# A small product moved from VectorE to GpSimd, transposes placed later among gate products, and a shorter conv norm sequence in a hybrid attention and convolution layer

## The chip, the cores and the metric

The kernel runs on one core of one Trainium2 chip. The metric is the device time of one execution in microseconds (us); lower is better. Engines are TensorE (matmuls and transposes, PE in the profile), VectorE (DVE), ScalarE (ACT), GpSimd (POOL) and SyncE (SP, which starts the DMAs).

## The reference

One pre-norm layer on x of 512 rows by 1024 columns, all float32. What the change touches lies in the token mixing:

```python
h = rms_norm(x, norm1_g)
proj = h @ w_in            # q, three K/V pairs, branch gates, conv input, merge gates
# compressed branch: softmax over 31 compressed keys, weighted by its branch gate
p_c = softmax(q . kc * scale - slope * dist) * valid ;  o_c = p_c @ vc
# selected and window branch (here all blocks are chosen: both are causal attention over 512 keys)
o = g0 * o_c + g1 * o_s + g2 * o_w ;   y_attn = o @ w_attn_br
# convolution branch
z = a * sigmoid(gate) ;  z = causal_dwconv(z, width 31) + b
z = silu(layer_norm(z)) ;  y_conv = z @ w_conv_br
x = x + (sigmoid(g_a) * y_attn + sigmoid(g_b) * y_conv) @ w_out
```

A gated convolution FFN and a final RMSNorm follow.

## The kernel before

Activations are held transposed, in 128 by 512 tiles. Every float32 operand is split into a rounded high part and a low part; a product is three matmuls, high by high (line 285), high weight by low activation (288) and low weight by high activation (291), each of 128x512. The weights' high parts are made by ScalarE (line 91) and the low parts by GpSimd or VectorE (line 93, tiles `wl`), from `raw` tiles that SyncE loads.

The attention runs in **16 steps** (lines 832 to 865): 8 heads by two branches, b = 0 for selected and b = 1 for window. Step s holds, on TensorE: `qk(s, 3)`, `qk(s, 2)` and `qk(s, 1)`, the scores of four row blocks (lines 739 and 744); `pv(s - 2)`, the value products (781, 786); and `ptr(s - 1, ...)`, the transposes of the probabilities of the step before, in three batches (768). Between them `fill(n)` puts n matmuls of the 480 of the merge gates' projection and of the convolution's output projection (`filler`, lines 605 to 615). TensorE's order is the order of the code (`manual_schedule`); the other engines' orders are set by a scheduler.

Behind each score tile VectorE finds the row maximum and subtracts (line 725, tile `p`), ScalarE takes the exponential and its sum (727), VectorE inverts the sum (754), and GpSimd scales the probabilities by it and by the branch gate (758, `soft`). Transposed probabilities leave their bank by ScalarE (771, `pt..h`) and VectorE (772, `pt..l`). Banks are few: two for scores (`s`), two for transposes (`t`), two for gate products (`mm`), one each for `o` and `y`. So the third batch of a step's transposes waits until both engines have emptied the bank of the first.

The compressed branch has its softmax in `cmp_scores` (lines 449 to 472), called for two halves before the steps: VectorE adds the distances, takes maxima and sums, inverts the sum (467) and multiplies it by the branch gate (470, `cst<-cst,gate`, 128x16); GpSimd applies the slope (464) and that product (471); ScalarE takes the exponential (465). `cmp_T` (474 to 484) transposes the result for four heads at a time, through the `t` banks (lines 479, 482, 483, tiles `pct`); both calls stand in step 2.

The convolution's 31 taps are VectorE work (508), fed out by `side(s)`, which is called six times a step. From step 6 on `side` advances `conv_norm` (645 to 691) by one `yield` per call: sums over channels (634 to 638), a mean by matmul (651), centring and squares (655, 656), sums of squares, a variance by matmul (663), a power on GpSimd (667), a scale spread by matmul (674), scaling (678 to 684) and the tiles `cB` (688, 689) that the convolution's output projection (`cb`) reads. Loops of empty `yield`s between them put calls between a VectorE result and the matmul that reads it.

Of the kernel before, what the change touches and what calls it, by code (L numbers as in the profile page):

```python
# [11 lines left out]
ALU = mybir.AluOpType  # L12
# [103 lines left out]
def hybrid_block_kernel(ctx: ExitStack, tc: tile.TileContext, x, norm1_g, w_in, cmp_pe_k, cmp_pe_v,  # L116
# [8 lines left out]
    act, vec, pool = nc.scalar, nc.vector, nc.gpsimd  # L125
# [6 lines left out]
    def big(name, shape=(P, 2, S), dt=F32):  # L132
        return sp.tile(list(shape), dt, tag="s", name=name)
# [140 lines left out]
    def psum(tag, name, pl=None):  # L274
        return psB.tile([P, S], F32, tag=tag, name=name, bufs=NB[tag])
# [173 lines left out]
    def cmp_scores(ib):  # L449
        pc = big(f"pc{ib}", (P, 2, 8, 32))  # L450
        st = bp.tile([P, 3, 16], F32, tag="cst", name=f"cst{ib}", bufs=2)
        pcf = pc.rearrange("p i h n -> p (i h) n")
        for ii in range(2):
            i = 2 * ib + ii
            ps = psum("st"[ib], f"sc{i}")
            pv = ps.rearrange("p (h a n) -> p h a n", h=8, a=2)
            for h in range(NH):
                mm(pv[:, h].rearrange("p a n -> p (a n)"), lhsT=QS[h // 2][:, h % 2, i * P : (i + 1) * P],
                   rhs=kc[:, h // 4].rearrange("p a n -> p (a n)"), start=True, stop=True)
            vec.tensor_tensor(pc[:, ii], pv[:, :, 1], ndc[:, i].unsqueeze(1).broadcast_to([P, 8, 32]), op=ALU.add)  # L460
            vec.tensor_tensor(pc[:, ii], pv[:, :, 0], pc[:, ii], op=ALU.add)
        vec.tensor_reduce(st[:, 0], pcf, axis=AX.X, op=ALU.max)
        vec.tensor_tensor(pcf, pcf, st[:, 0].unsqueeze(2).broadcast_to([P, 16, 32]), op=ALU.subtract)
        pool.tensor_tensor(pc, pc, sl.unsqueeze(1).unsqueeze(3).broadcast_to([P, 2, 8, 32]), op=ALU.mult)
        act.activation(pc, pc, AF.Exp)
        vec.tensor_reduce(st[:, 1], pcf, axis=AX.X, op=ALU.add)
        vec.reciprocal(st[:, 2], st[:, 1])
        gv = gate[:, 2 * ib : 2 * ib + 2].rearrange("p i (h b) -> p i h b", b=3)[:, :, :, 0]
        s2 = st[:, 2].rearrange("p (i h) -> p i h", i=2)
        vec.tensor_tensor(s2, s2, gv, op=ALU.mult)  # L470
        pool.tensor_tensor(pcf, pcf, st[:, 2].unsqueeze(2).broadcast_to([P, 16, 32]), op=ALU.mult)
        PC.append(pc)

# [2 lines left out]
    def cmp_T(hg):  # L476
        ps = psum("t", f"pct{hg}")
        for i in range(4):
            tr(ps[:, i * P : (i + 1) * P],
               PC[i // 2][:, i % 2, 4 * hg : 4 * hg + 4].rearrange("p h n -> p (h n)"), ident)  # L480
        pt_ = big(f"pct{hg}", dt=F32R)
        act.copy(pt_[:, 0], ps)
        vec.tensor_tensor(pt_[:, 1], ps, pt_[:, 0].bitcast(F32), op=ALU.subtract)
        PCT.append(pt_)
# [56 lines left out]
    for u in range(2):  # L541
        for i in range(2):
# [4 lines left out]
            for e in range(2):  # L547
                a, b = slice(64 * e, 64 * e + 64), slice(64 - 64 * e, 128 - 64 * e)
# [9 lines left out]
    for b in range(2):  # L558
# [4 lines left out]
        for g in range(2):  # L563
            kk = big(f"kk{b}{g}", dt=F32R)
            a, o_ = slice(64 * g, 64 * g + 64), slice(64 - 64 * g, 128 - 64 * g)
# [52 lines left out]
    left = [480]  # L618

    def fill(n):  # L620
        for _ in range(min(n, left[0])):
            next(fg)
            left[0] -= 1
# [21 lines left out]
    def conv_norm():  # L645

        yield from csum("sum")
        for _ in range(5):
            yield
        ps = psum("y", "cmean")  # L650
        mm(ps, lhsT=ones, rhs=cv["sum"], start=True, stop=True)
        yield
        for c in range(4):
            with pin():
                vec.tensor_tensor(zy[c][:, 0], zy[c][:, 1], ps, op=ALU.subtract)
                act.activation(zy[c][:, 1], zy[c][:, 0], AF.Square)
            yield
        yield from csum("sq")
        for _ in range(5):
            yield  # L660
        ps = psum("y", "cvar")
        for t in range(4):
            mm(ps[:, 2 * t : 2 * t + 2], lhsT=cv["sq"][:, t * P : (t + 1) * P], rhs=ones[:, 0:2], start=True, stop=True)
        rt = bp.tile([P, 8], F32, tag="crt", name="crt")
        dg = big("cdg", (P, 4, P))
        act.activation(rt, ps[:, :8], AF.Identity, bias=cst[:, 0:1])
        pool.tensor_tensor(rt, rt, cst[:, 1:2].broadcast_to([P, 8]), op=ALU.pow)
        for t in range(4):
            vec.tensor_scalar(dg[:, t], ident, rt[:, 2 * t : 2 * t + 1], 512.0, op0=ALU.mult, op1=ALU.mult)
        for _ in range(4):  # L670
            yield
        rs = psum("y", "crs")
        for t in range(4):
            mm(rs[:, t * P : (t + 1) * P], lhsT=ones, rhs=dg[:, t], start=True, stop=True)
        yield
        for c in range(4):
            with pin():
                vec.tensor_tensor(zy[c][:, 0], rs, zy[c][:, 0], op=ALU.mult)
                act.activation(zy[c][:, 0], zy[c][:, 0], AF.Identity, scale=lnh[:, c : c + 1],
                               bias=lnh[:, 4 + c : 5 + c])  # L680
            yield
            with pin():
                act.activation(zy[c][:, 1], zy[c][:, 0], AF.Tanh)
                vec.scalar_tensor_tensor(zy[c][:, 1], zy[c][:, 1], 1.0, zy[c][:, 0], op0=ALU.add, op1=ALU.mult)
            yield
            cb = big(f"cB{c}", dt=F32R)
            with pin():
                act.copy(cb[:, 0], zy[c][:, 1])
                pool.tensor_tensor(cb[:, 1], zy[c][:, 1], cb[:, 0].bitcast(F32), op=ALU.subtract)
            cB.append(cb)  # L690
            yield
# [138 lines left out]
    cmp_scores(1)  # L830
    fill(16)
    for s in range(16):
        n = left[0] - left[0] * (15 - s) // (16 - s) - (6 if s == 2 else 0)
        a = n // 4
        if s >= 1:
            soft(s - 1)
        qk(s, 3)
        side(s)
        fill(a - 1 if s else a + 2)
        qk(s, 2)  # L840
        side(s)
        fill(a if s else a + 6)
        qk(s, 1)
        side(s)
        if s >= 2:
            pv(s - 2)
        if s in (1, 9):
            padded(s // 9)
        if s == 2:
            cmp_T(0)  # L850
            fill(3)
            cmp_T(1)
            fill(3)
        if s >= 1:
            ptr(s - 1, [0])
        side(s)
        fill(a if s else 0)
        if s >= 1:
            ptr(s - 1, [1])
        side(s)  # L860
        fill(a if s else 0)
        if s >= 1:
            ptr(s - 1, [2, 3])
        side(s)
        fill(n - 4 * a + 1 if s else n - 2 * a - 8)
    assert left[0] == 0 and next(fg, None) is None and len(sig) == 16 and next(cn, None) is None


# [141 lines left out]
    for p in range(11):  # L1010
        tmp = {}
        for br, nm in enumerate("av"):
            tl = fp.tile([P, 2, S], F32, tag="ft", name=f"f{nm}{p}", bufs=3)
            tmp[nm] = tl
            for i in range(2):
# [9 lines left out]
                else:  # L1025
                    a = tmp["a"][:, i]
# [56 lines left out]
```

## Time and profile before

| | us |
|---|---|
| median of 3 runs (lowest to highest) | 748.64 (746.31 to 748.89) |
| the profiled execution's own time | 746.94 |
| its span in the trace | 745.2 |
| TensorE busy in the span | 727.0 |
| VectorE, ScalarE, GpSimd busy | 440.5, 335.8, 216.8 |

In the views below, a time is us from the span's start; a timeline row gives start and length of a run of equal instructions, how many there are, and in brackets how long the engine had been idle and on whom it waited. Matmuls are pipelined and their ends are modelled, so a run of equal matmuls is given with the modelled length of its last one; a single gate product of 128x512 is given as 0.39. PEclk is the clock granted to TensorE as a share of its full 2.4 GHz.

### The profile page before, as it was taken

How to read it: one execution, taken by the hardware profiler on the slowest of the kernel's cores; microseconds unless marked ns; L12 is line 12 of the kernel's file. 1: busy time of each engine (PE TensorE's matmuls, PEld its weight loads, DVE VectorE, ACT ScalarE, POOL GpSimd, SP SyncE). 2: the span in 40 equal slices, each digit the busy share in tenths (PEclk: the TensorE clock that was granted, in tenths of full speed). 3: DMA queues.
4: the chain of work that ended last, by engine and by line, in shares of the span. 5: the costliest groups of instructions: out<-in, count | busy, mean ns of one | idle time of the engine just before them, and what ended most of it. 6: DMA issues, size and time to landing. Idle time of an engine off the chain costs nothing.

```text
span 745.2 us, 9261 instructions
## 1 busy us (share of the span) xinstructions
PE 727.0 (98%) x3583; PEld 612.7 (82%) x3583; DVE 440.5 (59%) x755; ACT 335.8 (45%) x592; POOL 216.8 (29%) x168
## 2 busy tenths in 40 slices
PE   7999999889999999999999999999999999999995
PEld 7988889778878878788898888888888888888884
DVE  5479899989965656450358565656656564212225
ACT  6522576456567865342156434444443443112113
POOL 6544666565356664177330000000000000000001
PEclk9999999999999999999999999999999999999998
DMA  7442434211111111243433313322361332233102
GB/s 237 137 135 76 139 98 147 72 58 58 57 56 58 57 58 57 85 168 115 151 133 113 113 59 111 113 96 76 113 226 60 110 113 90 79 113 113 57 2 113
DMA packets 58613, 74.90 MB, mean 101 GB/s; under 512 B 2017, under 2 KB 48457, under 8 KB 58569
## 3 DMA queue, kind: packets, MB, share of 16 engines
q1 hardware_dynamic: 58569, 74.31, 29.9%
q8 instruction: 28, 0.46, 0.2%
q14 instruction: 16, 0.13, 0.1%
HBM read 70.11 MB, written 4.19 MB: 100 GB/s over the span
## 4 chain that ended last, share of the span: by engine, by line
PE 62%; issue 1%; DVE 0%; ACT 0%; POOLq 0%; POOL 0%
PE d0acc L936 16%; PE o0acc L936 6%; PE uv L285 5%; PE uv L291 5%; PE uv L288 5%; PE ua L291 5%; PE ua L285 5%; PE ua L288 5%; PE cb L291 1%; PE ab L885 1%; PE ab L889 1%; PE ab L887 1%; PE cb L288 1%; PE cb L285 1%; PE o L781 1%; PE t L768 1%
## 5 line engine op out<-in xcount | busy, mean ns | idle before, releaser
L91 ACT CAST wh<-raw 128x1024 fp32r<-128x1024 f32 (+1 forms) x114 | 117.5, 1036 | 195.9 <-PE d0acc L936 69.5
L93 DVE TENSOR_TENSOR wl<-raw,wh 128x1024 fp32r<-128x1024 f32 x62 | 75.7, 1223 | 129.3 <-PE d0acc L936 68.3
L93 POOL TENSOR_TENSOR wl<-raw,wh 128x1024 fp32r<-128x1024 f32 (+1 forms) x52 | 121.3, 2343 | 105.5 <-ACT wh L91 39.4
L1049 POOL TENSOR_TENSOR mf<-mf,cst 128x1 f32<-128x1 f32 x4 | 3.7, 931 | 356.1 <-DVE mf L1047 356.1
L936 PE MATMUL d0acc<-wh,act 128*128 128x512 f32 x352 | 86.9, 389 | 0.0
L508 DVE SCALAR_TENSOR_TENSOR cy<-zy,colB,cy 128x482 f32<-128x482 f32 (+28 forms) x116 | 85.0, 733 | 3.0 <-ACT cy L502 1.1
L936 PEld LDWEIGHTS d0acc<-wh,act 128*128 128x128 f32 x352 | 66.1, 188 | 13.7
L727 ACT ACTIVATE p<-p,st 128x512 f32<-128x512 f32 (+3 forms) x64 | 35.6, 558 | 28.9 <-DVE st L725 28.9
L936 PE MATMUL d0acc<-wl,act 128*128 128x512 f32 x176 | 47.0, 389 | 0.0
L285 PE MATMUL uv<-h,wh 128*128 128x512 f32 x176 | 44.4, 389 | 0.0
L758 POOL TENSOR_SCALAR p<-p,st,gate 128x512 f32<-128x512 f32 (+3 forms) x60 | 36.7, 630 | 25.4 <-DVE st L754 23.8
L288 PE MATMUL uv<-h,wh 128*128 128x512 f32 x176 | 43.5, 389 | 0.0
L291 PE MATMUL uv<-h,wl 128*128 128x512 f32 x176 | 43.5, 389 | 0.0
L285 PE MATMUL ua<-h,wh 128*128 128x512 f32 x160 | 39.5, 389 | 0.0
L291 PE MATMUL ua<-h,wl 128*128 128x512 f32 x160 | 39.5, 389 | 0.0
L288 PE MATMUL ua<-h,wh 128*128 128x512 f32 x160 | 39.5, 389 | 0.0
L288 PEld LDWEIGHTS uv<-h,wh 128*128 128x128 f32 x176 | 33.0, 188 | 6.9
L936 PEld LDWEIGHTS d0acc<-wl,act 128*128 128x128 f32 x176 | 33.0, 188 | 6.9
L291 PEld LDWEIGHTS uv<-h,wl 128*128 128x128 f32 x176 | 33.0, 188 | 6.9
L285 PEld LDWEIGHTS uv<-h,wh 128*128 128x128 f32 x176 | 32.6, 188 | 6.4
L285 PE MATMUL g<-h,wh 128*128 128x512 f32 x128 | 37.7, 417 | 0.0
L725 DVE CUSTOM_DVE_ANT_0 p<-s,nd 128x512 f32<-128x512 f32 (+3 forms) x64 | 29.8, 486 | 12.9 <-PE s L739 10.0
(386 smaller groups left out, 1438.7 us busy)
## 6 DMA issues: line engine op xcount, KB each, us to landing
raw<-in_ffn_w_up_dram SPq DMA_DIRECT2D x22, 1024.0 KB, 4.9
raw<-in_w_in_dram SPq DMA_DIRECT2D x11, 1024.0 KB, 4.9
raw<-in_ffn_w_down_dram SPq DMA_DIRECT2D x11, 1024.0 KB, 4.7
raw<-in_w_in_dram SPq DMA_DIRECT2D x10, 512.0 KB, 3.7
raw<-in_w_out_dram SPq DMA_DIRECT2D x4, 1024.0 KB
x<-in_x_dram SPq DMA_DIRECT2D x4, 512.0 KB, 7.2
raw<-in_w_conv_br_dram SPq DMA_DIRECT2D x2, 1024.0 KB, 4.8
raw<-in_w_attn_br_dram SPq DMA_DIRECT2D x2, 1024.0 KB
```

The source lines that it names most:

```text
L91: nc.scalar.copy(wh, src)
L93: eng.tensor_tensor(wl, src, wh.bitcast(F32), op=ALU.subtract)
L285: mm(ps, lhsT=wh[:, k, c : c + w], rhs=hs[k][:, 0], start=(k == 0), stop=False)
L288: mm(ps, lhsT=wh[:, k, c : c + w], rhs=hs[k][:, 1], start=False, stop=False)
L291: mm(ps, lhsT=wl[:, k, c : c + w], rhs=hs[k][:, 0], start=False, stop=(k == K - 1))
L508: vec.scalar_tensor_tensor(dst[:, s:], z[:, : S - s], colB[:, 4 * k + c : 4 * k + c + 1], y[:, s:], op0=ALU.mult, op1=ALU.add)
L725: last["ttr"] = vec.tensor_tensor_reduce(pi, src, nd[:, S - w :], scale=-SLOPE[h], scalar=3e38, op0=ALU.add, op1=ALU.min, accum_out=st[:, ...
L727: last["exp"] = act.activation(pi, pi, AF.Exp, scale=-1.0, bias=st[:, 0, i : i + 1], accum_out=st[:, 1, i : i + 1])
L758: (vec if s == 15 else pool).tensor_scalar(pi, pi, st[:, 2, i : i + 1], gate[:, i, gi : gi + 1], op0=ALU.mult, op1=ALU.mult)
L768: tr(ps[:, o_ : o_ + P], prob(s, i)[:, j * P : (j + 1) * P], ident)
L781: mm(po[:, j * P :], lhsT=VV[:, 2 * b + g, j].rearrange("p a d -> p (a d)"), rhs=PT[s][part][:, KO[j] : KO[j] + S - j * P], start=(b == 0 ...
L936: mm(accs[t][n], lhsT=acts(k)[:, ap, t * P : (t + 1) * P], rhs=w[:, 0, n * S : (n + 1) * S], start=st, stop=sp_)
```

## The change

Four edits. In `cmp_scores` the product of the inverse sum and the gate goes from VectorE to GpSimd. In step 1 six gate products are put ahead of the first batch of transposes, and fewer after it. Of the two `cmp_T` calls in step 2 the second goes to step 4, each followed by three gate products and, through `n`, three fewer in its step. In `conv_norm` the three runs of empty `yield`s go from 5, 5 and 4 to 3, 3 and 3.

```diff
         s2 = st[:, 2].rearrange("p (i h) -> p i h", i=2)
-        vec.tensor_tensor(s2, s2, gv, op=ALU.mult)
+        pool.tensor_tensor(s2, s2, gv, op=ALU.mult)
...
         yield from csum("sum")
-        for _ in range(5):
+        for _ in range(3):
             yield
...
         yield from csum("sq")
-        for _ in range(5):
+        for _ in range(3):
             yield
...
-        for _ in range(4):
+        for _ in range(3):
             yield
         rs = psum("y", "crs")
...
-        n = left[0] - left[0] * (15 - s) // (16 - s) - (6 if s == 2 else 0)
+        n = left[0] - left[0] * (15 - s) // (16 - s) - (3 if s in (2, 4) else 6 if s == 1 else 0)
...
-        if s == 2:
-            cmp_T(0)
+        if s in (2, 4):
+            cmp_T(s // 2 - 1)
             fill(3)
-            cmp_T(1)
-            fill(3)
+        if s == 1:
+            fill(6)
         if s >= 1:
             ptr(s - 1, [0])
         side(s)
-        fill(a if s else 0)
+        fill(a - (3 if s == 1 else 0) if s else 0)
         if s >= 1:
             ptr(s - 1, [1])
         side(s)
-        fill(a if s else 0)
+        fill(a - (2 if s == 1 else 0) if s else 0)
         if s >= 1:
             ptr(s - 1, [2, 3])
         side(s)
-        fill(n - 4 * a + 1 if s else n - 2 * a - 8)
+        fill(n - 4 * a + 1 + (5 if s == 1 else 0) if s else n - 2 * a - 8)
```

What the order of instructions becomes, at three places. A row is an instruction with its output and inputs; - is before, + is after.

GpSimd, around the compressed softmax (`cst` is the inverse sum, `pc` the probabilities, the numbers tell the two halves apart; `wl` is a low part of weights):

```order
 L93 TENSOR_TENSOR wl_1493<-raw_1289,wh_1492 128x1024
 L464 TENSOR_TENSOR pc_1381<-pc_1381,sl 128x512
+L470 TENSOR_TENSOR cst_1332<-cst_1332,gate 128x16
 L471 TENSOR_TENSOR pc_1331<-pc_1331,cst_1332 128x512
+L470 TENSOR_TENSOR cst_1382<-cst_1382,gate 128x16
 L471 TENSOR_TENSOR pc_1381<-pc_1381,cst_1382 128x512
```

The two products stand on GpSimd, each straight ahead of its reader; on VectorE, where each stood straight behind the inversion of line 467 and ahead of a line 725, nothing takes their place.

TensorE in step 1 (`g` are gate products, `s_1` the last scores of the step, `t_0` the first batch of transposes):

```order
+L739 MATMUL s_1_1530<-kk_1032,qs_791 128x256 x2
 L291 MATMUL g_1491<-h_0_115,wl_1366 128x512
 L291 MATMUL g_1491<-h_1_116,wl_1366 128x512
-L739 MATMUL s_1_1532<-kk_1032,qs_791 128x256 x2
-L768 MATMUL t_0_1547<-ident,p_1438 128x128
-L768 MATMUL t_0_1547<-ident,p_1440 128x128 x3
 L291 MATMUL g_1491<-h_2_117,wl_1366 128x512
 L291 MATMUL g_1491<-h_3_118,wl_1366 128x512
 L291 MATMUL g_1491<-h_4_119,wl_1366 128x512
 L291 MATMUL g_1491<-h_5_120,wl_1366 128x512
+L768 MATMUL t_0_1551<-ident,p_1438 128x128
+L768 MATMUL t_0_1551<-ident,p_1440 128x128 x3
```

The scores come two gate products earlier and the transposes four later. Counted over the step, the gate products after `s_3` were 5, then 6 after `s_2`, none between `s_1` and `t_0`, 6 after `t_0`, 6 after `t_1` and 4 after `t_2`; they are now 4, 5, 6, 2, 3 and 7.

VectorE in step 7, from the inverse sums of that step on; first before, then after (`sq` is the sum of squares of the conv norm, `of` the attention output, `pt6l` the low part of the transposed probabilities of step 6):

```order
L754 RECIPROCAL st_2054<-st_2054 128x4
L655 TENSOR_TENSOR zy_647<-zy_647,cmean 128x512
L794 TENSOR_TENSOR of_2163<-o_2064,of_2163 64x512
L772 TENSOR_TENSOR pt6l<-t_0_2168,pt6h 128x512
L772 TENSOR_TENSOR pt6l<-t_1_2183,pt6h 128x384
L634 TENSOR_TENSOR sq<-zy_504,zy_507 128x512
```

```order
L754 RECIPROCAL st_2054<-st_2054 128x4
L634 TENSOR_TENSOR sq<-zy_504,zy_507 128x512
L636 TENSOR_TENSOR sq<-sq,zy_584 128x512
L794 TENSOR_TENSOR of_2167<-o_2064,of_2167 64x512
L638 TENSOR_TENSOR sq<-sq,zy_647 128x512
L772 TENSOR_TENSOR pt6l<-t_0_2172,pt6h 128x512
```

The sums of squares, which stood behind the emptying of the first transpose banks, now stand ahead of it. The four centring instructions of line 655 moved forward as well, ahead of the step's second and third line 725. On TensorE the mean's matmul goes from behind `s_1` to behind `s_3` of step 7, the variance's from step 9 to the end of step 8, and the scale's from step 10 to step 9; SyncE's order stays as it was.

## Rows read from the trace of the kernel before

**Rows 1.** The page's first part: busy us, share of the span, instructions.

```profile
PE 727.0 (98%) x3583; PEld 612.7 (82%) x3583; DVE 440.5 (59%) x755; ACT 335.8 (45%) x592; POOL 216.8 (29%) x168
```

**Rows 2.** TensorE's waits: on whom, us in total, times, longest.

```profile
PE s L739 <- DVE st L725: 2.1, 2, 1.9
...
PE t L768 <- POOL p L758: 1.3, 1, 1.3
PE t L768 <- DVE pct L483: 1.0, 1, 1.0
PE cb L288 <- POOL cB L689: 1.0, 1, 1.0
...
PE t L768 <- DVE pt10l L772: 0.9, 1, 0.9
```

**Rows 3.** TensorE's timeline, end of step 0 and step 1.

```profile
138.61 1.98 PE L291 MATMUL g<-h,wl 128*128 128x512 f32 x8
142.47 0.50 PE L739 MATMUL s<-kk,qs 128*128 128x256 f32 x2 [1.88 <-DVE st L725]
...
143.13 3.19 PE L285 MATMUL g<-h,wh 128*128 128x512 f32 x7
...
151.26 0.66 PE L768 MATMUL t<-ident,p 128*128 128x128 f32 x4 [1.31 <-POOL p L758]
...
154.87 0.49 PE L768 MATMUL t<-ident,p 128*128 128x128 f32 x3
```

**Rows 4.** TensorE per microsecond: busy us (matmuls), granted clock, DMA share, GB/s.

```profile
144.00:145.00 1.00, 1.00 (x4) 0.50 1.05 375
```

**Rows 5.** VectorE's timeline around the compressed softmax and in step 1.

```profile
139.45 0.25 DVE L467 RECIPROCAL cst<-cst 128x16 f32<-128x16 f32 x1
139.80 2.00 DVE L470 TENSOR_TENSOR cst<-cst,gate 128x16 f32<-128x16 f32 x1
141.73 0.68 DVE L725 CUSTOM_DVE_ANT_0 p<-s,nd 128x512 f32<-128x512 f32 x1
...
144.10 0.67 DVE L466 TENSOR_REDUCE cst<-pc 128x16 f32<-128x512 f32 x1
...
145.10 0.18 DVE L470 TENSOR_TENSOR cst<-cst,gate 128x16 f32<-128x16 f32 x1
145.20 0.41 DVE L725 CUSTOM_DVE_ANT_0 p<-s,nd 128x256 f32<-128x256 f32 x1
...
152.57 0.69 DVE L772 TENSOR_TENSOR pt0l<-t,pt0h 128x512 fp32r<-128x512 f32 x1 [0.88 <-ACT pt0h L771]
```

**Rows 6.** GpSimd's timeline around the compressed softmax.

```profile
126.77 0.20 POOL L592 TENSOR_SCALAR_AFFINE_SELECT gate<-gate 128x8 f32<-128x8 f32 x1
...
138.92 2.85 POOL L93 TENSOR_TENSOR wl<-raw,wh 128x1024 fp32r<-128x1024 f32 x1 [1.74 <-issue]
141.72 1.05 POOL L464 TENSOR_TENSOR pc<-pc,sl 128x512 f32<-128x512 f32 x1
...
148.82 2.38 POOL L758 TENSOR_SCALAR p<-p,st,gate 128x512 f32<-128x512 f32 x4
```

**Rows 7.** ScalarE's timeline in the same stretch.

```profile
143.17 0.61 ACT L465 ACTIVATE pc<-pc 128x512 f32<-128x512 f32 x1
```

**Rows 8.** VectorE's timeline, steps 7 and 11.

```profile
216.57 0.69 DVE L772 TENSOR_TENSOR pt6l<-t,pt6h 128x512 fp32r<-128x512 f32 x1 [0.46 <-ACT pt6h L771]
...
218.37 2.81 DVE L634 TENSOR_TENSOR sq<-zy,zy 128x512 f32<-128x512 f32 x1
...
255.84 2.46 DVE L684 SCALAR_TENSOR_TENSOR zy<-zy 128x512 f32<-128x512 f32 x1
```

**Rows 9.** GpSimd's timeline, steps 7 and 8.

```profile
214.91 2.39 POOL L758 TENSOR_SCALAR p<-p,st,gate 128x512 f32<-128x512 f32 x4 [4.22 <-DVE st L754]
218.23 2.40 POOL L93 TENSOR_TENSOR wl<-raw,wh 128x1024 fp32r<-128x1024 f32 x1 [0.93 <-ACT pt6h L771]
```

**Rows 10.** TensorE's timeline, third batch of transposes in step 7.

```profile
217.93 0.49 PE L768 MATMUL t<-ident,p 128*128 128x128 f32 x3
```

## The prediction, made before the changed kernel was run

> **What bounds the kernel now.** I read the page first: TensorE is busy 98% of the span [rows 1], so the time can only fall where TensorE waits or runs slowly, and every other engine matters only as far as TensorE waits for it. Then the list of its waits [rows 2]: all the change aims at are there, four kinds and two single ones. The 2.1 on VectorE's line 725 are two waits, one of 1.9 and so a second of 0.2; then 1.3 on GpSimd's probabilities, 1.0 on `pct`, 1.0 on `cB`, 0.9 on `pt10l`. Together 6.3. Then TensorE's timeline where the longest lies [rows 3], and the same stretch by microseconds [rows 4]: behind the 1.88 wait the granted clock is 0.50, the lower level of 1.2 GHz, with matmuls back to back. Seven gate products are given as 3.19 there. At full clock eight are given as 1.98 with a last one of 0.39, so (1.98 - 0.39) / 7 = 0.23 each, and seven would be 6 x 0.23 + 0.39 = 1.77. The clock costs 1.4 on these, and by the same ratio about 0.25 on the score matmuls on both sides, 1.65 in all. So the one wait costs 3.5.
>
> Why it waits is in VectorE's timeline [rows 5]: the product of line 470 takes 2.00 the first time and 0.18 the second, on the same 128x16. The first ends at 141.80; GpSimd's low part of weights, begun at 138.92, ends at 141.77 [rows 6]. So VectorE stood still until GpSimd was done, and the row maximum queued behind the product, which frees TensorE's score bank, came at 141.73.
>
> The sum below is made against the profiled execution, 746.94, with its span of 745.2. That is 1.70 under the median of 748.64 and inside the runs' 746.31 to 748.89.
>
> **The product on GpSimd, and six gate products ahead of the transposes.** These act on one stretch and go together. Without line 470 the row maximum starts at 139.45 + 0.25 = 139.70 instead of 141.73 [rows 5]; with its 0.68 and a short read-out the bank is free at about 140.45. TensorE's eight products begun at 138.61 are through at 138.61 + 8 x 0.23 = 140.45. The wait and the slow clock go.
>
> What is late next: the other half of the softmax. GpSimd ends its weights at 141.77 as before and its line 464 at 142.77; ScalarE's exponential (0.61) follows at 142.85, not 143.17, where it queued behind that of the delayed row [rows 7]; VectorE's sum (0.67) and inversion (0.25) end at 144.4. Only then comes, on VectorE, the row maximum of the last scores of step 0, 0.41 and two smaller pieces of some 0.2 [rows 5], through at 145.2. TensorE wants that bank for `s_2` of step 1 at 140.45 + 0.5 (scores) + 7 x 0.23 + 0.46 + 4 x 0.23 = 143.9: a new wait of 1.3. The next two maxima queue behind it: `s_1` waits about 1.2, until 147.9.
>
> Then GpSimd: products at 142.8 and 144.4, each 0.20 by the nearest row, a 128x8 GpSimd instruction [rows 6]; bounds 0 (if it runs while GpSimd waits anyway) and 1.05, what GpSimd takes for 128x512. The second line 471 ends at 145.65, the weights, 2.40 as in rows 9, at 148.05, the scaling of step 0's probabilities at 150.45; before, it was 148.82 + 2.38 = 151.20 [rows 6]. Each 0.1 on the second product moves this by 0.1. A rule of the Trainium skill speaks against this edit: "GPSIMD Engine Reference", section "3.1 Elementwise — side-by-side cycle accounting", keeps elementwise work on VectorE, with GpSimd 1.96 times slower; by it the product would take 0.18 x 1.96 = 0.35, an estimate, and the sum would be 0.15 higher, as only the second one counts. No run here shows that product on GpSimd.
>
> TensorE, with 4 + 5 + 6 = 15 gate products after `s_3` instead of 11, would be at the transposes at 147.9 + 0.24 + 6 x 0.23 = 149.5 and waits 1.0 for the scaling, to 150.5 instead of 151.26. It has done four more products by then: 0.76 + 4 x 0.23 = 1.68 won. Part of it goes back: only five products, not twelve, stand between the first batch and the third, whose bank ScalarE and VectorE must empty first. Before, that was done at 152.57 + 0.69 = 153.26 [rows 5], 2.0 after the first batch began; I put 2.4, as step 1's exponentials now fall closer to it on ScalarE. So the third batch starts at 152.9 after a wait of 0.65; before it started at 154.87 [rows 3] with three more products done. 154.87 - 152.9 - 3 x 0.23 = **1.3 won**. Bounds: nothing, if the queue on VectorE is longer by as much as I found it shorter; and 4.8, all of 1.88 + 1.65 + 1.31, if TensorE waits nowhere. I take the reckoned value, since each link of it is a row here.
>
> **`cmp_T` split.** In step 2 the first transposes no longer find both banks full, so the 1.0 goes [rows 2]. The second batch now takes the bank that `pct` leaves; VectorE is there about 0.2 after TensorE wants it. **0.8 won**, bounds 0 and 1.0. In step 4 the other call puts the same pattern; there six gate products (1.4) stand between the first and the second batch as well, and VectorE has no chain of the softmax behind it. I cost that at nothing; without cover it is the same 1.0. The gate products that change places are as many as before: nothing.
>
> **Conv norm shortened.** Five calls fewer, of six to a step: the last `cB` comes most of a step earlier, and TensorE's 1.0 for it goes. The 0.9 on `pt10l` came from a blocked line 684, 2.46 long [rows 8], at a place that it leaves; the 0.2 in step 8 from the sum of squares, 2.81 long [rows 8], blocked by the weights from 218.23 [rows 9]. So 2.1 go. What comes: in step 7 the sums of squares stand ahead of `pt6l`. TensorE wants its bank at 217.93 [rows 10]; `pt6l` began at 216.57. Now ScalarE has all four squares ahead of the copy, some 0.6 each as line 465 takes for that width [rows 7], and VectorE three sums of nearly 0.7 and, beside GpSimd's scaling from 214.91 to 217.30 [rows 9], some blocking. I reckon `pt6l` from 218.5 to 219.1: a wait of 1.2. For the two later places where a blocked line 684 stands ahead of `pt8l` and `pt9l` I put 0.4 together. **0.5 won** (2.1 - 1.2 - 0.4). Bounds: 2.1, and 2 lost, if at both of two places a blocked sum of 2.5 is waited for in full less what I counted. I stand near the middle, since these blocks are short where GpSimd runs its four scaling pieces and long only beside the weights.
>
> **Sum:** 746.94 - 1.3 - 0.8 - 0.5 = **744.3**.
>
> **Rivals.**
> *All of it is collected*: GpSimd's and VectorE's chains are shorter than I reckon, TensorE waits for neither in step 1. Then 1.88 + 1.65 + 1.31 + 1.0 and half the conv norm's 2.1 go: 6.9, so 740.0. For it: the six products give 1.4 of cover. Against it: the scaling cannot end before about 150.4 by rows 6, whatever TensorE does.
> *The gain is given back in place*: the four waits of step 1, each about 1, close together, bring the clock down again, as one of 1.88 did [rows 3, 4], and step 7 costs as much as is saved later. The slow clock costs up to 1.4, of which the wait for the scaling hides 1.0. Then 1.3 - 0.4 and 0.8 stay, less 0.8 lost in the conv norm: 746.0. For it: the order moves VectorE's work ahead of what frees banks. Against it: waits of 1.31 and less are followed by full clock in this trace.
> *Slower*: the conv norm's sums and line 684 are blocked by GpSimd while `pt6l`, `pt8l` and a later one queue behind them. Price by rows 8: 2.46 and 2.81 are 1.9 and 2.2 more than such an instruction takes unblocked. It decides from where TensorE waits 1.88 or more, since then 1.65 comes on top. At three places, 3 x (2.0 + 1.65) = 10.95, less the 2.1 saved there and 2.1 in the first steps: 6.8 slower, 753.7. The Trainium skill, "SBUF — State Buffer", section "SBUF: two separate sides", has the rule: VectorE's instruction with two inputs there and GpSimd's take a shared port whole, and whoever begins first blocks the other. By that rule rows 5 and 6 agree (2.00 against 0.18), and this rival is open at every such sum. Against it: in the trace of before, line 470 apart, no wait of TensorE above 0.9 came of such a block [rows 2].
> *The change does not reach its bound*: if the 2.00 was not GpSimd's doing, the row maximum stays late. Then the four products more ahead of the first batch cover 0.9 of its 1.31, 0.4 goes back at the third, and with 0.8 and 0.5 it is 745.1.
>
> **How the numbers follow.** About 0.5%, 3.7, is what a measurement of this kernel can tell from no change; against the median of 748.64 that is 744.9. Chances: the forecast's case 0.43, giving 743 to 745.3, three quarters of it under 744.9; all collected 0.16; given back 0.28; the maximum stays late 0.08; slower 0.05. Faster by over 0.5% is 0.32 + 0.16 + 0.02 = 0.50, slower 0.04, no change 0.46. The range runs from 741.0, between the full gain and the forecast, to 748.2: the given-back case with the 1.95 by which the slowest run of before stands over the profiled one.
>
> **What would show it.** In the changed trace: line 470 on GpSimd at about 0.2, no VectorE instruction of 2.0 near 140; the wait before the last scores of step 0 gone and the clock at 1.00 from 140 to 147; TensorE waiting about 1 each for `s_2`, `s_1` and the first batch of step 1; no wait on `pct` above 0.3 and none on `cB`; a wait of about 1.2 on `pt6l`. The prediction is wrong if the scaling of step 0 ends well before 150.3 or after 151, if the clock falls in step 1, or if the conv norm's part shows waits of over 2.

## The result, and the profile after

The changed kernel takes **744.01 us** (median; 743.80 to 744.63), against 748.76 (746.31 to 748.89) for the kernel before in the same comparison: ratio **0.9946, 95% interval 0.9924 to 0.9967**, faster by 0.54% by the ratio (the medians alone differ by 0.63%). Forecast were 744.3 and a range of 741.0 to 748.2, with 0.50 on faster by over 0.5%; the interval reaches from 0.33% to 0.76%, so whether the gain is over 0.5% stays open.

The profiled execution took 743.80 with a span of 742.1, 3.1 less than that of before. Of this 0.83 has nothing to do with the change: the first score matmul of step 0 already starts that much earlier, and nothing ahead of it was edited. The rest lies in the sixteen steps. These are the two ends of that stretch in TensorE's timeline, the first score of step 0 and the first product of the attention's projection. Of the kernel before:

```profile
135.07 0.62 PE L739 MATMUL s<-kk,qs 128*128 128x512 f32 x2
...
305.89 0.48 PE L885 MATMUL ab<-oT,wh 128*128 128x512 f32 x1
```

and of the changed kernel, with the rows of steps 0 and 1 that answer to [rows 3]:

```profile
134.24 0.62 PE L739 MATMUL s<-kk,qs 128*128 128x512 f32 x2
...
139.60 0.40 PE L739 MATMUL s<-kk,qs 128*128 128x256 f32 x2
...
140.07 1.78 PE L285 MATMUL g<-h,wh 128*128 128x512 f32 x7
...
144.43 0.58 PE L739 MATMUL s<-kk,qs 128*128 128x384 f32 x2 [1.22 <-DVE st L725]
...
146.97 0.50 PE L739 MATMUL s<-kk,qs 128*128 128x256 f32 x2 [0.80 <-DVE st L725]
...
149.76 0.65 PE L768 MATMUL t<-ident,p 128*128 128x128 f32 x4 [0.91 <-POOL p L758]
...
151.91 0.55 PE L768 MATMUL t<-ident,p 128*128 128x128 f32 x3
...
302.69 0.49 PE L885 MATMUL ab<-oT,wh 128*128 128x512 f32 x1
```

The stretch was 305.89 - 135.07 = 170.82 and is 302.69 - 134.24 = **168.45: 2.37 less**, where the forecast reckoned 2.6. "The stretch" below is always this one; it leaves out the start, which differs between executions.

The last scores of step 0 no longer wait (1.88 before), and the seven gate products behind them take 1.78 where they took 3.19. In place of the one long wait stand three of 1.22, 0.80 and 0.91. TensorE in stretches of 2 us (busy us, matmuls, granted clock, DMA share, GB/s) shows the same:

```profile
143.00:145.00 2.00, 0.78 (x4) 1.00 1.07 379
145.00:147.00 2.00, 1.20 (x7) 1.00 0.19 65
147.00:149.00 2.00, 1.86 (x8) 1.00 0.00 0
```

There is idle time but no slow clock: 1.00, which is 2.4 GHz, against the 0.50 of [rows 4].

VectorE's timeline around the compressed softmax, to be held against [rows 5], and four rows from around the conv norm's scaling:

```profile
138.55 0.24 DVE L467 RECIPROCAL cst<-cst 128x16 f32<-128x16 f32 x1
138.71 0.63 DVE L725 CUSTOM_DVE_ANT_0 p<-s,nd 128x512 f32<-128x512 f32 x1
...
235.84 0.69 DVE L684 SCALAR_TENSOR_TENSOR zy<-zy 128x512 f32<-128x512 f32 x1 [0.18 <-ACT zy L683]
...
238.21 2.74 DVE L798 TENSOR_TENSOR oT<-of,oT 128x512 fp32r<-128x512 f32 x1 [1.06 <-ACT oT L797]
...
246.21 2.56 DVE L684 SCALAR_TENSOR_TENSOR zy<-zy 128x512 f32<-128x512 f32 x1 [2.04 <-ACT zy L683]
...
248.78 0.65 DVE L772 TENSOR_TENSOR pt9l<-t,pt9h 128x512 fp32r<-128x512 f32 x1
```

and GpSimd's, against [rows 6]:

```profile
138.00 2.89 POOL L93 TENSOR_TENSOR wl<-raw,wh 128x1024 fp32r<-128x1024 f32 x1 [1.74 <-issue]
140.86 1.04 POOL L464 TENSOR_TENSOR pc<-pc,sl 128x512 f32<-128x512 f32 x1
141.87 0.22 POOL L470 TENSOR_TENSOR cst<-cst,gate 128x16 f32<-128x16 f32 x1
...
144.96 2.38 POOL L93 TENSOR_TENSOR wl<-raw,wh 128x1024 fp32r<-128x1024 f32 x1
147.32 2.38 POOL L758 TENSOR_SCALAR p<-p,st,gate 128x512 f32<-128x512 f32 x4
...
238.01 2.40 POOL L93 TENSOR_TENSOR wl<-raw,wh 128x1024 fp32r<-128x1024 f32 x1
...
245.83 2.39 POOL L93 TENSOR_TENSOR wl<-raw,wh 128x1024 fp32r<-128x1024 f32 x1 [2.86 <-PE g L291]
```

The maximum of line 725 now starts right behind the inversion; the product takes 0.22 on GpSimd, behind the weights that it used to wait for on VectorE. The scaling ends at 147.32 + 2.38 = 149.70, which is what the first transposes wait for.

TensorE's waits, against [rows 2]:

```profile
PE s L739 <- DVE st L725: 2.3, 3, 1.2
...
PE t L768 <- DVE pt9l L772: 1.4, 1, 1.4
PE t L768 <- POOL p L758: 0.9, 1, 0.9
...
PE t L768 <- DVE pt6l L772: 0.9, 1, 0.9
```

`pct`, `cB` and `pt10l` are gone, as is the 1.9. But `pt9l` and `pt6l` are new, and of the 2.3 on line 725 a third part, 0.3, comes later, between those two (at 242.54): the shortened norm has waits of its own. The 0.3 follows line 798, the attention output's low part, which takes 2.74 from 238.21 beside the weights of 238.01 and has the last low parts of `pt8l` and the next row maximum queued behind it.

### The profile page after: what moved, and what is told of

Read it like the earlier page. It is cut to its first block, busy times and chain, and to the rows that moved or that the text cites. A ratio compares the mean times of both kernels' runs of the same rounds, so it can differ in the third digit from the quotient of the medians.

```text
span 742.1 us, 9260 instructions
## 1 busy us (share of the span) xinstructions
PE 725.1 (98%) x3583; PEld 611.4 (82%) x3583; DVE 437.5 (59%) x753; ACT 336.3 (45%) x592; POOL 218.3 (29%) x170
## 4 chain that ended last, share of the span: by engine, by line
PE 75%; DVE 2%; ACT 2%; POOL 1%; issue 1%; POOLq 0%; ACTq 0%; DVEq 0%
PE d0acc L936 16%; PE o0acc L936 6%; PE uv L285 5%; PE uv L291 5%; PE uv L288 5%; PE ua L291 5%; PE ua L288 5%; PE ua L285 5%; PE g L288 2%; PE g L291 2%; PE o L781 2%; PE g L285 2%; PE t L768 2%; PE s L739 2%; PE cb L291 1%
## 5 line engine op out<-in xcount | busy, mean ns | idle before, releaser
L758 POOL TENSOR_SCALAR p<-p,st,gate 128x512 f32<-128x512 f32 (+3 forms) x60 | 38.2, 652 | 27.0 <-DVE st L754 19.8
```

Source lines behind the costliest of these rows:

```text
L758: (vec if s == 15 else pool).tensor_scalar(pi, pi, st[:, 2, i : i + 1], gate[:, i, gi : gi + 1], op0=ALU.mult, op1=ALU.mult)
```

## The experiments

Each part was first run alone on the kernel before, then the parts together with one left out, then the port by itself, and last three tries for more. The table has the parts; the stretch and the waits of steps 0 and 1 (before the last scores of step 0 or the two later scores of step 1, and before the first transposes) are from one profiled execution of each; how far a stretch differs from one execution to the next was not measured. Each ratio is to the runs of before in its own comparison, and these differ: median 748.76 (4 runs) for the change, 747.70 (31) for the four parts alone, 747.80 (17) for product and six, all but the norm, the port on the kernel before and the thirteen more, 747.61 (9) for all but the product and the rest.

| kernel | median us (lowest to highest) | ratio to before, interval | stretch | waits | lowest clock in the steps |
|---|---|---|---|---|---|
| before | 748.76 (746.31 to 748.89) | | 170.82 | 1.88; 1.31 | 0.50 behind 1.88 |
| the change | 744.01 (743.80 to 744.63) | 0.9946 (0.9924 to 0.9967) | 168.45 | 1.22, 0.80; 0.91 | 1.00 |
| product alone | 747.42 (746.55 to 748.31) | 1.0007 (0.9998 to 1.0016) | 171.50 | 1.04, 0.57; 2.31 | 0.50 behind 2.31 |
| six alone | 745.47 (745.23 to 746.55) | 0.9982 (0.9971 to 0.9992) | 169.96 | 1.83; 0.38 | 0.50 behind 1.83 |
| split alone | 746.70 (746.54 to 747.74) | 0.9996 (0.9986 to 1.0007) | 171.29 | 1.92; 2.56 | 0.50 behind 2.56 |
| norm alone | 747.97 (746.34 to 749.08) | 1.0006 (0.9994 to 1.0018) | 172.40 | 1.74; 2.56 | 0.50 behind 2.56 |
| product and six | 744.79 (744.53 to 745.72) | 0.9957 (0.9942 to 0.9971) | 169.10 | 0.91, 0.79; 0.91 | 1.00 |
| all but the product | 744.77 (744.29 to 745.34) | 0.9962 (0.9949 to 0.9976) | 168.85 | 1.73, 0.26; 1.16 | 1.00 |
| all but the norm | 744.03 (743.66 to 744.69) | 0.9942 (0.9930 to 0.9954) | 168.21 | 1.12, 0.79; 0.91 | 1.00 |

### The product alone, and the six alone

Of the change only the first edit, and only the second:

```diff
-        vec.tensor_tensor(s2, s2, gv, op=ALU.mult)
+        pool.tensor_tensor(s2, s2, gv, op=ALU.mult)
```

> Only the product of line 470 goes to GpSimd. Stretch from the first scores of step 0 to the first matmul of the attention projection: 170.8 us in the kernel before, 168.45 with all four edits. Theory (the 2.00 was GpSimd's doing, and behind it the softmax of step 0 is bound by GpSimd and VectorE): line 470 takes 0.2 on GpSimd, the 1.88 wait and the half clock behind it go, but TensorE then waits at s_2 and s_1 of step 1 about 1 us each and over 2 us for the scaled probabilities of step 0, whose end comes only 0.8 earlier; net 0.8 won if the clock stays full, up to 0.6 lost if the wait of over 2 brings it to half: stretch 170.0 to 171.4. Rival (no second chain): the 1.88 and the 1.65 of slow clock are won in full, stretch 167.3.

```diff
+        if s == 1:
+            fill(6)
         if s >= 1:
             ptr(s - 1, [0])
```

> Only the six gate products ahead of step 1's transposes (with fewer behind them). Theory: the 1.88 wait and the half clock stay; the four products more cover 0.9 of the 1.31 wait for the scaled probabilities, and 0.4 comes back as a wait of the third batch for the emptied bank: stretch 170.3 (0.5 won). Rival (the cover is worth all of it): 1.3 won, 169.5; rival (the third batch gives all back): 170.8 or more.

Product alone: TensorE's timeline at the first transposes of step 1, and the same place by 2 us:

```profile
149.94 1.12 PE L768 MATMUL t<-ident,p 128*128 128x128 f32 x4 [2.31 <-POOL p L758]
```

```profile
149.00:151.00 2.00, 1.06 (x5) 0.57 0.00 0
151.00:153.00 2.00, 2.00 (x7) 0.57 0.00 0
```

The 1.88 is gone, as reckoned, and TensorE arrives sooner where it then waits for GpSimd's scaling: 2.31 instead of 1.31, with the clock at half behind it. Nothing is won: the stretch is 171.50, 0.1 beyond the 171.4 expected for a clock at half, and the interval of the ratio holds 1. Six alone: the wait of 1.83 with the slow clock behind it stays, the one for the scaling shrinks to 0.38, and a third of the change's gain is there by the ratio; of the stretch 170.82 - 169.96 = 0.86 is won, between the expected 0.5 and its rival's 1.3. So the product needs the six: it takes a wait away, and they cover what then stands open. The six alone win half of what the two win together.

### The split alone, and the norm alone

```diff
-        if s == 2:
-            cmp_T(0)
-            fill(3)
-            cmp_T(1)
+        if s in (2, 4):
+            cmp_T(s // 2 - 1)
```

> Only the second compressed transposition moved from step 2 to step 4. Theory: the wait of 1.0 on pct in step 2 goes and nothing comes in step 4: stretch 169.7 to 169.9 (0.9 to 1.1 won). Rival (the same wait comes back at the second batch of transposes in step 2 or in step 4): 170.8.

```diff
-        for _ in range(5):
+        for _ in range(3):
```

(twice, and the third from 4 to 3)

> Only the conv norm's shorter runs of empty yields. Theory (from the trace of the changed kernel): the waits on cB, pt10l and the 0.2 in step 8, 2.1 together, go, and waits on pt6l (0.9), on a row maximum (0.3) and on pt9l (1.4) come: 0.5 lost, stretch 171.3. Rival (my prediction's 0.5 won): 170.3; rival (all 2.1 won, the new waits belonging to other edits): 168.7.

Split alone: the wait on `pct` is gone. Norm alone: the waits on `cB`, `pt10l` and the 0.2 are gone; `pt9l` 1.4, `pt6l` 0.9 and a 0.3 have come, as in the changed kernel. Both ratios' intervals hold 1. Both missed the stretches expected, 169.7 to 169.9 and 171.3, by 1.4 and 1.1.

These two leave steps 0 and 1 as they were, and yet in both the slow clock lies elsewhere, which is what was missed. Norm alone, TensorE's timeline and its 2 us stretches:

```profile
141.55 0.50 PE L739 MATMUL s<-kk,qs 128*128 128x256 f32 x2 [1.74 <-DVE st L725]
...
150.35 0.66 PE L768 MATMUL t<-ident,p 128*128 128x128 f32 x4 [2.56 <-POOL p L758]
```

```profile
143.00:145.00 2.00, 2.00 (x10) 1.00 1.08 383
...
151.00:153.00 2.00, 2.00 (x7) 0.53 0.00 0
153.00:155.00 2.00, 2.00 (x8) 0.62 0.00 0
```

Behind the first wait the clock stayed at 1.00, so TensorE was at the transposes earlier and waited 2.56 there instead of 1.31. From the first score of step 0 to those transposes it is 16.06 (150.35 - 134.29), in the kernel before with its slow clock 151.26 - 135.07 = 16.19, and with the split alone, also at full clock there, 150.55 - 134.31 = 16.24: **the slow stretch of [rows 3, 4] cost next to nothing**, since the scaling came no sooner. Behind the wait for the scaling nothing hides it: the stretch is 172.40 against 170.82, of which some 0.2 is the norm's own (below).

### The parts together

The change without its norm; the product and the six with neither split nor norm; and the change with the product of line 470 left on VectorE.

> The changed kernel with the convolution norm's waits of 5, 5 and 4 yields put back. Theory (the shortened norm lost 0.5 us in the changed kernel's trace: 2.1 of waits on cB, pt10l and one more were replaced by 0.9 + 1.4 + 0.3): TensorE's waits on pt6l (0.9), pt9l (1.4) and the 0.3 before an L739 go, cB 1.0 and pt10l 0.9 come back with about 0.2; the time is 0.3 to 0.7 us below the changed kernel, 743.2 to 743.8. Rival (the forecast, 0.5 us won by the shortened norm): 0.5 us above it, 744.4 to 744.7. Second rival: the half clock behind one of the waits decides and the time falls back by over 1.5 us.

> The kernel before with the product on GpSimd and the six gate products ahead of the first transposes of step 1, and neither the split nor the norm. Theory (these two need each other: the product takes the maximum of L725 from behind 2.00 us, the six products fill what then stands open before the transposes): the wait of 1.9 and that of 2.6 are both gone, no wait in 139 to 152 is over 1.3 us, the granted clock is 1.00 throughout that stretch, and the time is 744.2 to 745.2, well under the sum of the two alone (+0.5 - 1.3). The wait on pct (1.0), cB (1.0) and pt10l (0.9) stay. Rival (the parts only add): 746.5 to 747.3 with a stretch of half clock behind one of the waits.

> The changed kernel with the product of L470 back on VectorE: six products ahead, split and shortened norm stay. Theory (each of the product and the six fills alone leaves one wait of 1.8 to 2.4 us, and behind it TensorE goes at half clock for some 3.4 us): the product again takes about 2.0 us on VectorE, the wait before an L739 of step 1 is again 1.7 to 2.0 us with granted clock 0.50 behind it, and the time is that of the six fills alone less at most the split's 0.8: 744.8 to 745.6. Rival (the product on GpSimd does nothing, as it did alone): 743.7 to 744.4, the changed kernel's time.

The product and the six together give 0.9957, most of the change's 0.9946, where alone they gave 1.0007 and 0.9982. In 139 to 152 no wait is over 0.91 and the clock is 1.00, as that theory wanted. The 1.0 of step 2 is still there, 0.99 at the same place, though the view puts it down to GpSimd's line 758. The stretch splits the gain: 170.82 - 169.10 = **1.72** for the two, 169.10 - 168.21 = **0.89** for the split, and 168.21 - 168.45, **0.24 lost**, for the norm. TensorE's waits of the kernel without the norm in 158 to 303:

```profile
PE cb L288 <- POOL cB L689: 1.0, 1, 1.0
PE t L768 <- DVE pt10l L772: 0.9, 1, 0.9
PE o L781 <- DVE pt14l L772: 0.4, 1, 0.4
PE s L739 <- DVE st L725: 0.2, 1, 0.2
```

2.1 of these are what the norm removes, and its own are 0.9 + 1.4 + 0.3 = 2.6: by the waits 0.5 lost, by the stretch 0.24. In the time the norm is nothing: 744.03 without, 744.01 with, in two comparisons. The expected 0.3 to 0.7 in favour of leaving it out is not there.

Without the product the two rows at its place are these, on VectorE and on TensorE:

```profile
139.94 2.00 DVE L470 TENSOR_TENSOR cst<-cst,gate 128x16 f32<-128x16 f32 x1
```

```profile
142.61 0.50 PE L739 MATMUL s<-kk,qs 128*128 128x256 f32 x2 [1.73 <-DVE st L725]
```

The wait is back, but in this execution the clock behind it is 1.00, so that part of the expectation fell. The time, 744.77, is just under the band of 744.8 to 745.6. The slow clock is elsewhere in this trace, ahead of anything edited: behind two short waits of TensorE near the start, where fifteen matmuls take 3.26 (1.83 in the changed kernel). Two rows of TensorE's timeline, and one of its view by microseconds:

```profile
7.37 0.30 PE L244 MATMUL n1a<-ident,xn_n1a 128*128 128x128 f32 x1 [0.93 <-DVE xn_n1a L235]
8.57 3.26 PE L244 MATMUL n1a<-ident,xn_n1a 128*128 128x128 f32 x15 [0.90 <-DVE g1c L314]
```

```profile
9.00:10.00 1.00, 1.00 (x7) 0.50 1.01 410
```

So step 0 starts at 135.36 here, 1.1 later than in the changed kernel. The stretch leaves that out: given the six, the product is worth 168.85 - 168.45 = 0.40 of it.

### The port by itself

Is it GpSimd that VectorE waits for in line 470? The product stays on VectorE, but one of its inputs lies in PSUM:

```diff
-        vec.reciprocal(st[:, 2], st[:, 1])
+        ri = psum("o", f"ri{ib}")[:, :16]
+        vec.reciprocal(ri, st[:, 1])
...
-        vec.tensor_tensor(s2, s2, gv, op=ALU.mult)
+        vec.tensor_tensor(s2, ri.rearrange("p (i h) -> p i h", i=2), gv, op=ALU.mult)
```

> The kernel before with one edit: the reciprocal of L467 goes into a PSUM bank instead of SBUF, so that the product of L470 stays on VectorE but reads only one operand from SBUF. Theory (an instruction of VectorE with two SBUF inputs waits for the port that GpSimd holds): the product takes 0.15 to 0.35 us instead of 2.00 though GpSimd's L93 lies beside it, and the maximum of L725 starts about 1.7 us sooner, as in the changed kernel; the time is that of the product alone, 747 to 748. Rival (the 2.00 us are a wait on data, or any VectorE instruction waits beside GpSimd): the product stays at 1.5 to 2.1 us and the time is that of the kernel before.

VectorE and GpSimd in that kernel (line 471 is line 470 of before, one line lower):

```profile
138.08 0.68 DVE L463 TENSOR_TENSOR pc<-pc,cst 128x512 f32<-128x512 f32 x1
138.68 0.26 DVE L468 RECIPROCAL ri<-cst 128x16 f32<-128x16 f32 x1
139.04 0.17 DVE L471 TENSOR_TENSOR cst<-ri,gate 128x16 f32<-128x16 f32 x1
139.13 0.68 DVE L726 CUSTOM_DVE_ANT_0 p<-s,nd 128x512 f32<-128x512 f32 x1
```

```profile
138.13 2.89 POOL L93 TENSOR_TENSOR wl<-raw,wh 128x1024 fp32r<-128x1024 f32 x1 [1.74 <-issue]
```

0.17 instead of 2.00, in the middle of GpSimd's 2.89. So it was the two SBUF inputs, and neither data nor the engine. The time is 746.98 (745.34 to 747.31), just under the expected 747 to 748, ratio 0.9981 (0.9970 to 0.9991), the stretch 171.51, that of the product alone (171.50). Here too a wait of 2.27 for the scaling has the slow clock behind it.

In the kernel without the norm, the same edit in place of the product on GpSimd:

> The changed kernel with the norm's yields put back, and the product of L470 on VectorE again, but with the reciprocal in PSUM, so that it reads one operand from SBUF. Theory (it matters only that the product does not wait for GpSimd, not on which engine it lies): about 0.2 us for the product, no wait over 1.3 us in step 1, clock 1.00 there, and the time of the kernel with the norm put back, 743.6 to 744.4. Rival (GpSimd is better placed, since the pcf product behind it is GpSimd's own): 744.5 to 745.2.

743.84 (743.68 to 744.49), ratio 0.9952 (0.9937 to 0.9968), the stretch 168.21, to the hundredth that with the product on GpSimd; no wait over 1.25. On which engine the product lies made no difference here, only that it does not stand still.

### Tries for more

Thirteen more gate products in step 1, to cover the three waits that are left:

```diff
-        fill(a - 1 if s else a + 2)
+        fill(a - 1 + (5 if s == 1 else 0) if s else a + 2)
...
-        fill(a if s else a + 6)
+        fill(a + (4 if s == 1 else 0) if s else a + 6)
...
-            fill(6)
+            fill(10)
```

> The changed kernel with the norm's 5, 5 and 4 yields put back, and 13 more gate products taken from later steps into step 1: five behind the first score, four behind the second, four more ahead of the first transposes. Theory (TensorE is idle for 1.22 + 0.80 + 0.91 us in this step because nothing else stands in its queue, and the 13 products of 0.235 us cover that, while steps 2 to 15 have about one product fewer each and few waits): the three waits fall to under 0.3 us each, and the time is 1.5 to 2.9 us below the kernel with the norm put back alone, 740.5 to 742.3. Rival (the products are missed later: the wait on cB grows by about the products that its place has moved forward, up to 2 us, and the transposes of later steps wait for GpSimd): within 0.7 us of it, or slower.

745.54 (743.96 to 748.80), ratio 0.9968 (0.9955 to 0.9981): worse than the 744.03 without them, though the stretch of its trace is only 302.96 - 134.35 = 168.61 against 168.21. The three waits are gone, and two others are there, in TensorE's timeline:

```profile
154.40 0.55 PE L768 MATMUL t<-ident,p 128*128 128x128 f32 x3 [2.36 <-DVE pt0l L772]
...
264.42 0.50 PE L285 MATMUL cb<-cB,wh 128*128 128x512 f32 x1 [3.22 <-ACT cB L688]
```

The convolution's projection comes sooner than its data, as the rival had it. And VectorE's order has changed: three taps in a row stand ahead of what empties the transposes' bank.

```profile
151.46 2.30 DVE L508 SCALAR_TENSOR_TENSOR cy<-zy,colB,cy 128x508 f32<-128x508 f32 x3
153.66 0.68 DVE L772 TENSOR_TENSOR pt0l<-t,pt0h 128x512 fp32r<-128x512 f32 x1
```

Last, the weights' subtraction that stands ahead of the scaling on GpSimd (144.96 in the changed kernel) is issued behind it, without the norm, with the product on GpSimd and then on VectorE with PSUM. The part of the edit shown issues it; the rest, not shown, keeps it back in the weights' queue until then:

```diff
             soft(s - 1)
+        if s == 1:
+            W.hold = False
+            W.dma_to(W.halves[29]["u"])
+            with tc.issue_after(last["pr"].ins):
+                W._half(29)
+            W.n_half = 30
```

> The changed kernel with the norm's yields put back, and one weight half's subtraction (L93, 2.38 us on GpSimd at 144.96, between the pcf products and the scaling of step 0) placed behind that scaling. Theory (the first transposes of step 1 wait for L758, which starts only when L93 ends, 1.4 us after its reciprocal at about 145.9): L758 starts at 145.9 to 146.3, the first transposes start about 1.0 us sooner, and the time falls by 0.5 to 1.2 us against the kernel with the norm put back, to 742.6 to 743.5. Rival (VectorE is busy throughout 146 to 156 and sets the pace; the wait moves to pt0l): unchanged within 0.3 us. Second rival (three L93 in a row make the scaling of step 1 late and the second step's transposes wait): 0.5 to 2 us slower.

> The two edits before together: the subtraction placed behind the scaling, and the product on VectorE with its reciprocal in PSUM. Theory: the two lie on different engines and add, so the time is that of the kernel with the deferred subtraction within 0.4 us. Rival: the product's place on VectorE puts the maximum of L725 later and takes the gain of the deferred subtraction away, 743.6 to 744.4.

743.21 (743.05 to 744.17), ratio 0.9944 (0.9932 to 0.9957), and 743.59 (743.04 to 743.92), 0.9945 (0.9933 to 0.9958). The stretches are 167.75 and 167.57, the shortest of all. GpSimd in the first (lines stand three lower):

```profile
145.37 2.39 POOL L761 TENSOR_SCALAR p<-p,st,gate 128x512 f32<-128x512 f32 x4 [2.35 <-DVE st L757]
147.72 7.10 POOL L94 TENSOR_TENSOR wl<-raw,wh 128x1024 fp32r<-128x1024 f32 x3
```

and TensorE at the third batch of transposes:

```profile
151.50 0.55 PE L771 MATMUL t<-ident,p 128*128 128x128 f32 x3 [1.14 <-DVE pt0l L775]
```

Three subtractions stand in a row behind the scaling: not only that of 144.96 went there, as meant, but also the one that stood at 138.00, beside the compressed softmax. So the scaling came sooner than the expected 145.9, these two runs do not tell the two subtractions apart, and no weights stand beside the product any more. The scaling starts 2 us sooner and the first transposes 1.5, but of these 0.46 is left at the end of the stretch (168.21 - 167.75), since the third batch now waits 1.14 for VectorE, which is busy without a gap from 146 on. Medians and stretches are the lowest of the study; the intervals of the ratios lie on that of the change, so better than the change is not shown.

## Why the prediction was right

**The sum was nearly right, two of its three terms a little small, and the third of the wrong sign.** That 2.6 and 2.37 lie so close is in part luck: the terms are off by 0.42 and 0.09 one way and by 0.74 the other. Product and six: 1.3 reckoned, 1.72 in the stretch. The links were as reckoned: waits of 1.22, 0.80 and 0.91 where 1.3, 1.2 and 1.0 were put; the product 0.22 where 0.20 was put; at the first transposes (151.26 - 0.83) - 149.76 = 0.67 and four products of 0.23, 1.59, where 1.68 was put. What was put too high is what goes back at the third batch: its wait of 0.65 is not among the waits, and by its start (154.87 - 0.83) - 151.91 - 3 x 0.23 = 1.44 are won. That is the changed kernel's trace; the 1.72 is that of the two alone, where the first of the three waits was 0.91 instead of 1.22, which is the 0.3 between them. Split: 0.8 reckoned, 0.89 measured. The scaling ended at 149.70, which by the start of before is 150.53, inside the 150.3 to 151 that were named.

**The step that failed is the conv norm's "0.5 won".** The 2.1 went as it said, and `pt6l` costs 0.9 where 1.2 was put. But "the two later places where a blocked line 684 stands ahead of `pt8l` and `pt9l` I put 0.4 together" measured nothing at `pt8l`, where line 684 was not blocked (0.69 at 235.84), and 1.4 at `pt9l`: there line 684 took 2.56 beside the weights of 245.83, and the transposes waited for the rest of it. The 0.3 came of another blocked instruction, line 798, which the prediction did not have. A wait of a known mechanism was counted at under a third of its size, and the term has the other sign: 0.24 lost in the stretch, nothing in the time. The two parts alone, both with the slow clock in the open, agree with the 0.24: 172.40 - (171.29 + 0.89) = 0.22.

**"So the one wait costs 3.5" was wrong for this execution.** The 1.65 of slow clock were hidden behind the scaling, as the norm alone and the split alone show (16.06 and 16.24 against 16.19 to the transposes). The sum escaped it because it followed GpSimd's chain to the transposes and did not subtract 3.5. The rival "all collected" added the 1.65 and came to 740.0; even with the subtractions deferred, the lowest run is 743.04. Two figures of the prediction are off without moving the sum: 746.0 and 1.95 make 748.0, not 748.2, at the upper end of the range, and the blocked 2.46 and 2.81 are 1.8 and 2.1 above unblocked ones (0.69), not 1.9 and 2.2.

**Why the medians differ by more than the traces.** The forecast started from an execution of 746.94 and came out near the median of after, though that of before is 748.76. Without the 0.83 by which its start was late (its clock was 1.00 there), that execution would have taken 746.1; the profiled execution of the norm alone, whose slow clock lies behind the wait for the scaling, took 747.80 with a stretch longer by 172.40 - 170.82 = 1.58. In the comparison of the four parts the runs of before fall into groups of 746.1 to 746.6, 747.7 to 748.0 and 748.5 to 748.9. The first two are some 1.4 apart, which is what the slow clock cost in the open there (1.58 less the norm's 0.2). The third lies 0.9 above the second, and its runs have a lower mean clock (0.992 to 0.994, against 0.994 and 0.995 in the other two), so a late start at full clock does not explain it. A second slow stretch would, such as the one at 9 to 12 in the trace of all but the product, which put step 0 back by 1.1. That these groups are where the slow clock fell is argued from the profiled executions and the mean clocks; the other runs have no trace. If so, most executions of before paid for the slow clock in the open (14 of the 31 lie in the first group, one of the 4 in the first comparison, and none of the 17 and 9 in the others), and the changed kernel, in which no wait of the steps is over 1.4, is freed of it: its runs lie within 0.83. The stretch accounts for 2.37 us, 0.32%, of the 0.54%; that the rest is a matter of these groups is argued, not shown.

**The rivals.** "The maximum stays late" is refuted by the rows of line 725. "Given back in place" did not occur in the trace: the clock was 1.00 in all the steps. "Slower" by blocked sums: the Trainium skill's rule ("SBUF — State Buffer", section "SBUF: two separate sides") holds here in both halves. With two SBUF inputs line 470 takes 2.00 beside GpSimd, with one 0.17; and GpSimd's weights take 2.89 instead of 2.39 where line 463, with two SBUF inputs, began 0.05 ahead of them. Its price was paid once, 1.4 at `pt9l` of the 1.87 by which line 684 was longer (2.56 - 0.69), beside the smaller waits of 0.9 and 0.3, not three times. The other page of the Trainium skill, "GPSIMD Engine Reference", section "3.1 Elementwise — side-by-side cycle accounting", gave an estimate of 0.35 by its ratio of 1.96; the 128x16 product takes 0.22 on GpSimd and 0.17 to 0.18 on VectorE unblocked, a ratio of about 1.25, so for this small product the ratio does not hold.

## What to carry to other kernels

A wait that is taken away matters only as far as the next engine's chain lets its waiter go on, so reckon every chain to the point where they meet, here the scaling ahead of the transposes (alone, the product won nothing and the six 0.18%; together they won 0.43%, each against the runs of before in its own comparison). A small VectorE instruction with two SBUF inputs can stand until the GpSimd instruction beside it ends (here 2.00 instead of 0.18); give it one input in PSUM, or put it on GpSimd, and look at each such place that a change moves, since the cost of a blocked instruction is that of what is queued behind it. Filling a wait with work from later only pays if that work's data is there in time and the waiter is not held by a full engine.

## What the runs showed that was not expected

- **The same wait may or may not bring the slow clock.** Behind waits of 1.88, 1.83, 2.27, 2.31, 2.56 and 2.56 the granted clock was 0.50, which is 1.2 GHz; behind others of 1.73, 1.74, 1.92, 2.36 and 3.22 it stayed at 1.00. No wait of 1.39 or less in steps 0 to 15 had it, but near the start two short ones close together, 0.93 and 0.90, did in one trace. So a long wait is a risk that shows in the scatter of the runs: those of the kernel with waits of 2.36 and 3.22 lie between 743.96 and 748.80, the traced one, 744.05, with a mean clock of 0.997, the slowest with 0.991.
- **A slow clock can be free.** In the kernel before, 1.4 us lost on seven products were time that TensorE would have stood waiting 4 us later.
- **The blocked product ended when GpSimd's weights ended.** With the product left on VectorE, it ended at 141.94 by its row (139.94 + 2.00); GpSimd's weights of 2.86, begun at 139.05, ended at 141.91.
